# One decoder layer on one core: the left tiles start 128 bytes later, the last output products get written-out places, and the first weights take another queue

## The chip, the cores and the metric

The kernel runs on one core of one Trainium2 chip. A core has five engines that run side by side: TensorE (PE; its weight loads are listed apart as PEld), VectorE (DVE), ScalarE (ACT), GpSimd (POOL) and SyncE (SP), which here only issues transfers. Each executes its own instructions in a fixed order and waits for the others by semaphores. Data lies in an on-chip memory of 128 partitions, matmul results in eight banks of 512 float32 values per partition (PSUM). The metric is the device time of one execution in microseconds (us), as the median of several runs.

## The reference

A hybrid decoder layer on x of 1024 rows (the sequence) by 1024 columns, in float32:

```
xn = rmsnorm(x, attn_norm_g)
proj = xn @ w_in                      # 1024 x 2312, cut into qa ka va qb kb vb f_logit
out_a = swa_sinks_attention(...)      # 8 heads of 64, window 128, 2 key heads, sinks, ALiBi
out_b = forgetting_attention(...)     # 8 heads of 64, causal, bias c[t] - c[s], c = cumsum(log f)
x = x + concat(out_a, out_b) @ w_out
hn = rmsnorm(x, mlp_norm_g)
hid = square(relu(hn @ w_up))         # 1024 x 4096
y = x + hid @ w_down
```

q and k are normalised per head before the scores.

## The kernel before

**Arithmetic.** Every float32 operand of a large product is split in two parts of the type float32r (`split`, line 73, one engine for the high part and one for the remainder), and a product is three matmuls: high by high, high by low, low by high (`mm`, line 70). The stationary operand (the weights, loaded by PEld before each matmul) is the second argument, the streamed operand the third. The up and the down projection use seven block products where eight would be usual.

**Order.** The kernel is written as one program. A planner then simulates a time line and fixes the order of each engine's instructions: it takes what is ready by its own simulation, in program order unless `tc.high_priority` puts a piece ahead (`prep` does). `tc.issue_after(i)` keeps the instructions of a block behind instruction i in that order. So a place in the program is a wish, and `issue_after` is a bound.

**Stages.**
1. *Start* (lines 161 to 196): for each of eight slices k of the inner dimension, SP loads half of xT, the first weights `w_a0`, and the other half (lines 171 to 173); ACT and DVE split x into `xh` and `xl`, DVE and POOL split the weights; PE multiplies into `qps`. `vt`, the tile of small vectors, comes over ACT's own queue (line 105), and ACT's function table is loaded behind it (line 106).
2. *Heads* (lines 203 to 778): a unit is the scores of one head for some rows (`scores_a`, `scores_b`) and, two units later (`DEPTH`), its mixing with v (`mix_a`, `mix_b`: transposes `tpb`, evictions `pth` on ACT and `ptl` on DVE, products `pvb`, the sum `mtb`). `pend` holds the units whose mixing is still to come; `drain(n)` writes the mixing of all but the last n. Between the units lie fillers: projections `ps` of the next heads and the first half of the output projection (`out_first`). `marks` holds the last matmul of each unit's scores. The last heads' rows come in the order `ORDER_END`, 1, 3, 0, 2, in quarters of 256 columns.
3. *Output projection* (lines 789 to 930): eight column tiles dt, each the sum over eight tiles e of the mixed heads. Tiles 0 to 3 are summed early and kept in `part_d`; tiles 4 to 7 come last. Tiles 0 to 6 go through memory (`split_mix` writes `mixs_d`, `load_mix` reads it); tile 7 is split directly from `mtb` (line 708). The products of one dt with one tile are six matmuls of 128x512 (`out_products`). dt 0 and dt 4 have their products with tiles 4 to 6 ahead of the last two units' mixing (lines 863 to 872), then `drain(0)`, then tile 7. `out_finish` adds the part from `part_d`, stores h, and makes the sums and splits that the up projection streams (`bh`, `bl`). For dt 7 the part is loaded into `rr`, a tile of its own.
4. *Up* (`up`, line 978): 16 steps of seven products, 84 matmuls of 128x512 each: weights `wu` stationary, `bh` and `bl` streamed, out to `pu`.
5. *Down* (`down`, line 1102): weights `wx` stationary, `hx` streamed, out to `pd`, in sets of two tiles (`down_set`), 24 matmuls of 128x512 a set. `FIRST` says that the first and third set lie left, the second and fourth right; all later ones lie left.

**Where tiles lie.** Pools on the left side grow upwards from the small constants (`cp`), pools on the right grow downwards from the end. Each tile takes its bytes per partition, rounded up to 32. Ahead of the left tiles stand 2176 bytes of the system's own and, in cp, ident 512, ident_b 256, ones1 32, vt 160 (144 rounded up), nsnk, gqk, rstd and ep2 32 each, rqk 192, nm_a and dn_a 256 each, dn_b 128, mask_b 256, rt and the two of `rsqrt` 32 each, and before 256: together 4704, which is 18 x 256 + 96. `xh`, `xl` and all tiles of zl (mix, wos, wu, hx, wx and others) have sizes that are multiples of 256, so all start at 96 in a step of 256 bytes (the weights of the projections, 1568 bytes each, turn through all multiples of 32). The right side ends at 229,344, 895 x 256 + 224, and so the tiles of ap1 (qk, v) and zr (`bh`, `bl`, the right sets of the down stage) start at 224. In ap2 small tiles lie between the large ones: the tiles of k (`k1`, `k2z`), `pth`, `ptl` and the scores start at 192, the tiles of q (`q1`) at 64.

Of the kernel before, what the change touches and what calls it, by code (L numbers as in the profile page):

```python
# [8 lines left out]
F32 = mybir.dt.float32  # L9
# [7 lines left out]
P = 128  # L17
# [3 lines left out]
NT = S // P  # L21
HD = 64
NH = 8
# [30 lines left out]
def hybrid_layer(  # L54
# [13 lines left out]
    nc = tc.nc  # L68

    def mm(out, lhsT, rhs, start, stop):  # L70
        return nc.tensor.matmul(out, lhsT, rhs, start=start, stop=stop)  # L71
# [20 lines left out]
    cp = ctx.enter_context(tc.tile_pool(name="cp", bufs=1))  # L92
# [10 lines left out]

    vt = cp.tile([P, 36], F32, name="vt")
    nc.scalar.dma_start(vt, vecs)
    nc.scalar.preload_act_table_set("natural_log_exp_and_others")
    ga, gm, vec, bfb, snk = (
# [32 lines left out]
    at = ExitStack()  # L140
    ap1 = at.enter_context(tc.tile_pool(name="ap1", bufs=1, side="right"))
    ap2 = at.enter_context(tc.tile_pool(name="ap2", bufs=1, side="right"))
    maskd = ap2.tile([P, P], F32, tag="mt", name="maskd", bufs=2)
    nc.gpsimd.memset(maskd, 0.0)
# [23 lines left out]
    for k in range(KT):  # L168
        xr = ap2.tile([P, S], F32, tag="s", name="xr", bufs=NS)
        wr, wh, wl = w_tiles()  # L170
        nc.sync.dma_start(xr[:, halves[0]], xT[k * P : (k + 1) * P, halves[0]])
        nc.sync.dma_start(wr[:, :384], w_a0[:, k, :])
        nc.sync.dma_start(xr[:, halves[1]], xT[k * P : (k + 1) * P, halves[1]])
# [54 lines left out]
    def qknorm(x, nh, tlo, thi, r=None):  # L228
# [8 lines left out]
        ss, r0, u = (  # L237
            ap2.tile([P, 16], F32, tag=tag, name=tag, bufs=2)[:, : n * nh]
            for tag in ("ss", "sr0", "su")
# [16 lines left out]
        if r is None:  # L256
            rv = ap2.tile([P, 16], F32, tag="r", name="r", bufs=2)[:, : n * nh]
            rv = th(rv)
        else:
            rv = r[:, tlo:thi, :]  # L260
# [32 lines left out]
    marks = []  # L293

    def paced():
        return tc.issue_after(marks[-1]) if marks else nullcontext()
# [126 lines left out]
    def forget_gates():  # L423
# [31 lines left out]
        )  # L455
        offs = ap2.tile([NH * NT, 1], F32, name="offs")
        nc.vector.tensor_copy(offs, off[: NH * NT, 0:1])
# [167 lines left out]
    def scores_b(p, qp, h):  # L625
        q1, k1, k2, cb = heads[p, "q"][h], heads[p, "k1", h], k2_of[h], heads[p, "cb", h]
        probs = []
        for i in (2 * qp, 2 * qp + 1):
# [4 lines left out]
            )  # L633
            nm = ap2.tile([P, 4], F32, tag="nm", name="nmb", bufs=4)
            dn = ap2.tile([P, 4], F32, tag="dn", name="dnb", bufs=4)
            qs = q1[:, i * P : (i + 1) * P]
# [34 lines left out]
    def mix_b(probs, p, qp, h):  # L671
        r = slice(h * HD, (h + 1) * HD)
        pv = pa.tile([P, 512], F32, tag="pv", name="pvb", bufs=2)
        for b in range(qp + 1):
# [18 lines left out]
            for par in range(2):  # L693
                st = heads[p, "v", h][:, 2 * b + par, :]
                mm(pvo, st, hv[:, :, 1 - par, :], b == 0 and par == 0, False)
                mm(pvo, st, lv[:, :, 1 - par, :], False, diag and par == 1)
        tmp = ap2.tile([HD, 512], F32, tag="cmb", name="tmpb", bufs=1)
# [11 lines left out]

    qkb = {}  # L710
    mh, ml, mixt = {}, {}, {}
    pend = []
# [5 lines left out]
    def drain(n):  # L718
        while len(pend) > n:
            prep(pend.pop(0))  # L720
# [87 lines left out]
    def load_mix(e):  # L808
        mix_tiles(e)
        nc.sync.dma_start(mixt[e].bitcast(F32), mixs_d[e].rearrange("c p s -> p c s"))  # L810
# [50 lines left out]
    fill(True)  # L861
    load_mix(6)
    ahead_of = []
    for dt in (0, 4):
        w = out_weights(dt, 4)

        ps = first_banks() if dt == 0 else [
            pa.tile([P, 512], F32, tag="sc", name=f"po{c}", bufs=2) for c in range(2)
        ]
        with paced():  # L870
            out_products(ps, w, range(4, 7))
        ahead_of.append((dt, ps, w))
    drain(0)
    for dt, ps, w in ahead_of:
        out_products(ps, w, [7])
# [25 lines left out]
    def out_finish(dt, ps):  # L901
        t, gain = dt % 4, gm[:, dt : dt + 1]
        h = slot(f"w{2 + dt // 4}", "h", [S]) if dt < 7 else rr
        part["load"] = nc.sync.dma_start(h, part_d[dt])
        for c, cs in enumerate((left, right)):
# [381 lines left out]
```

## Time and profile before

| | us |
|---|---|
| median of 3 runs | 1126.16 (1122.52 to 1127.7) |
| profiled execution, its own time | 1124.34 |
| its span, from the first to the last instruction | 1122.6 |
| mean granted TensorE clock | 0.998 |

The profile comes from one further execution. Its span is cut into the busy times of each engine; idle time of an engine is put down to what released it at its end (a transfer, another engine's result). A matmul's listed duration reaches from its start to its modelled end and overlaps the next one; what counts in a dense stretch is the distance from one start to the next. The chain of waits follows the work that ended last backwards, from each instruction to what it waited for. By stages: the start reaches to about 40 us, heads and fillers to about 464, the rest of the output projection to about 512, up to 813, down to the end.

### The profile page before, as it was taken

To read this page: it belongs to the slowest core of one execution; us is meant where nothing else is said; L and a number is where in the kernel's file an instruction comes from. 1 tells how busy PE (TensorE), PEld (TensorE's weight loads), DVE (VectorE), ACT (ScalarE), POOL (GpSimd) and SP (SyncE) were. 2 spreads that over 40 slices of the span, in tenths; PEclk is the share of its full clock that TensorE was granted. 3 is DMA by queue.
4 is the path that set the end of the run, shared out by engine and by line. 5 is a ranking of instruction groups with operands and counts; after the bars stand their busy time and mean duration, and the time that the engine had idled before them with its cause. 6 is when DMAs were issued, how large, how long until landed. Compare 5 with 4: busy or idle time off the path is not lost.

```text
span 1122.6 us, 15570 instructions
## 1 busy us (share of the span) xinstructions
PE 1098.7 (98%) x5551; PEld 937.5 (84%) x5551; DVE 765.4 (68%) x1311; ACT 575.4 (51%) x1013; POOL 361.0 (32%) x338
## 2 busy tenths in 40 slices
PE   9999998999999999899999999999999999999998
PEld 8999988799997888777888887888888888888886
DVE  7476665765667577699867677855575876674395
ACT  5567557766677656455454534344444433333331
POOL 4751613335434545124232323222221222222100
PEclk9999999999999999999999999999999999999999
DMA  9311302314438656473454544335699786665523
GB/s 312 124 36 37 95 24 59 96 29 142 153 120 312 203 182 219 168 236 131 173 194 169 196 151 159 134 121 194 227 392 351 258 299 244 216 230 205 173 95 113
DMA packets 95710, 195.68 MB, mean 174 GB/s; under 512 B 7136, under 2 KB 19088, under 8 KB 95632
## 3 DMA queue, kind: packets, MB, share of 16 engines
q1 hardware_dynamic: 95488, 194.66, 49.6%
q8 instruction: 44, 0.72, 0.3%
q14 instruction: 34, 0.28, 0.1%
q10 hardware_dynamic: 144, 0.02, 0.0%
HBM read 141.61 MB, written 53.04 MB: 173 GB/s over the span
## 4 chain that ended last, share of the span: by engine, by line
PE 83%; DVE 7%; issue 4%; DMA 4%; POOL 1%; ACT 1%; SPq 0%; DVEq 0%; ACTq 0%; POOLq 0%
PE pd L71 27%; PE pu L71 27%; PE ps L71 12%; PE po L71 4%; PE qps L71 3%; PE spb L71 3%; PE pvb L71 2%; PE tpb L683 2%; PE sp L71 1%; DVE ptl L360 1%; DMA mixs_d<-mixs 1%; DVE sb L647 1%; DVE bl L78 1%; PE pv L71 1%; DMA wr<-in_w_b_dram 1%
## 5 line engine op out<-in xcount | busy, mean ns | idle before, releaser
L71 PE MATMUL pd<-hx,wx 128*128 128x512 f32 x1344 | 304.9, 389 | 0.0
L71 PEld LDWEIGHTS pd<-hx,wx 128*128 128x128 f32 x1344 | 252.3, 188 | 52.4
L71 PE MATMUL pu<-bh,wu 128*128 128x512 f32 x896 | 281.6, 395 | 0.8 <-ACT wu L75 0.8
L71 PEld LDWEIGHTS pu<-bh,wu 128*128 128x128 f32 x896 | 168.8, 188 | 40.7 <-ACT wu L75 1.2
L71 PE MATMUL pu<-bl,wu 128*128 128x512 f32 x448 | 176.9, 395 | 0.5 <-DVE bl L78 0.5
L75 ACT CAST hx<-hr 128x1024 fp32r<-128x1024 f32 x56 | 59.0, 1054 | 176.2 <-PE pd L71 171.3
L78 POOL TENSOR_TENSOR wx<-wda,wx 128x1024 fp32r<-128x1024 f32 x24 | 64.5, 2687 | 197.0 <-ACT wx L75 197.0
L78 DVE TENSOR_TENSOR hx<-hr,hx 128x1024 fp32r<-128x1024 f32 x56 | 72.7, 1305 | 73.5 <-ACT hx L75 73.4
L71 PE MATMUL ps<-wh,xh 128*128 128x384 f32 (+1 forms) x320 | 110.2, 345 | 0.3 <-ACT qkb L600 0.3
L71 PE MATMUL ps<-wh,xl 128*128 128x384 f32 (+1 forms) x320 | 109.3, 342 | 0.0
L71 PE MATMUL ps<-wl,xh 128*128 128x384 f32 (+1 forms) x320 | 109.1, 342 | 0.0
L71 PEld LDWEIGHTS pu<-bl,wu 128*128 128x128 f32 x448 | 84.4, 188 | 21.1 <-DVE bl L78 0.9
L71 PE MATMUL po<-mix,wos 128*128 128x512 f32 x384 | 95.8, 400 | 3.7 <-DMA mix<-mixs_d 1.6
L78 POOL TENSOR_TENSOR wu<-wus,wu 128x512 fp32r<-128x512 f32 x32 | 48.0, 1501 | 133.4 <-ACT wu L75 133.4
L71 PEld LDWEIGHTS po<-mix,wos 128*128 128x128 f32 x384 | 70.9, 190 | 18.3 <-DMA mix<-mixs_d 1.8
L75 ACT CAST wu<-wus 128x512 fp32r<-128x512 f32 x64 | 39.0, 618 | 79.4 <-PE pu L71 76.0
L78 POOL TENSOR_TENSOR wu<-wur,wu 128x512 fp32r<-128x512 f32 x32 | 43.3, 1354 | 88.2 <-ACT wu L75 88.2
L360 DVE TENSOR_TENSOR ptl<-tpb,pth 128x512 fp32r<-128x512 f32 (+1 forms) x80 | 50.0, 632 | 25.9 <-ACT pth L359 25.2
L965 DVE TENSOR_TENSOR ht<-hb 128x512 f32<-128x512 f32 x32 | 21.8, 722 | 64.7 <-ACT hb L1020 64.7
L78 POOL TENSOR_TENSOR wl<-wr,wh 128x384 fp32r<-128x384 f32 (+1 forms) x47 | 49.9, 1076 | 48.8 <-ACT wh L75 36.9
L75 ACT CAST wx<-wda 128x1024 fp32r<-128x1024 f32 x56 | 58.3, 1044 | 7.2 <-DMA wda<-in_w_d_dram 6.6
L71 PEld LDWEIGHTS ps<-wh,xh 128*128 128x128 f32 x320 | 60.4, 189 | 1.1 <-ACT qkb L600 0.6
(218 smaller groups left out, 2058.4 us busy)
## 6 DMA issues: line engine op xcount, KB each, us to landing
wda<-in_w_d_dram SPq DMA_DIRECT2D x34, 1024.0 KB, 9.0
hr<-hid_d SPq DMA_DIRECT2D x56, 512.0 KB, 5.8
wur<-in_w_u_dram SPq DMA_DIRECT2D x32, 512.0 KB, 4.4
hid_d<-ht SPq DMA_DIRECT2D x16, 1024.0 KB, 4.3
hid_d<-hb SPq DMA_DIRECT2D x16, 768.0 KB, 3.6
mixs_d<-mixs SPq DMA_DIRECT2D x14, 512.0 KB, 3.4
mix<-mixs_d SPq DMA_DIRECT2D x7, 1024.0 KB, 8.7
wr<-in_w_b_dram SPq DMA_DIRECT2D x32, 192.0 KB, 2.4
```

Source lines behind the costliest of these rows:

```text
L71: return nc.tensor.matmul(out, lhsT, rhs, start=start, stop=stop)
L75: hi_eng.copy(hi, src)
L78: lo_eng.tensor_tensor(out=lo, in0=src, in1=hi.bitcast(F32), op=ALU.subtract)
L360: nc.vector.tensor_tensor(out=lo[:, cols], in0=pt[:, cols], in1=hi[:, cols].bitcast(F32), op=ALU.subtract)
L647: nc.vector.tensor_tensor_reduce(out=pr[:, c * 512 : c * 512 + n], in0=sp[:, :n], in1=cb[:, c * 512 : c * 512 + n], scale=1.0, scalar=3e38 ...
L683: nc.tensor.transpose(tp[:, c0 : c0 + P], probs[qi][:, kb * P : (kb + 1) * P], ident)
L965: eng.tensor_tensor(out=out, in0=a, in1=b, op=ALU.subtract)
```

## The change

```diff
--- before.py
+++ after.py
@@ -101,9 +101,10 @@
     ones1 = cp.tile([P, 1], F32, name="ones1")
     nc.vector.memset(ones1, 1.0)
 
-    vt = cp.tile([P, 36], F32, name="vt")
-    nc.scalar.dma_start(vt, vecs)
-    nc.scalar.preload_act_table_set("natural_log_exp_and_others")
+    vt = cp.tile([P, 68], F32, name="vt")
+    nc.scalar.dma_start(vt[:, :36], vecs)
     ga, gm, vec, bfb, snk = (
         vt[:, a:b] for a, b in ((0, 8), (8, 16), (16, 20), (20, 28), (28, 36))
     )
@@ -140,6 +141,8 @@
     at = ExitStack()
     ap1 = at.enter_context(tc.tile_pool(name="ap1", bufs=1, side="right"))
     ap2 = at.enter_context(tc.tile_pool(name="ap2", bufs=1, side="right"))
+    ap3 = at.enter_context(tc.tile_pool(name="ap3", bufs=1, side="right"))
     maskd = ap2.tile([P, P], F32, tag="mt", name="maskd", bufs=2)
     nc.gpsimd.memset(maskd, 0.0)
     nc.gpsimd.affine_select(
@@ -169,7 +172,9 @@
         xr = ap2.tile([P, S], F32, tag="s", name="xr", bufs=NS)
         wr, wh, wl = w_tiles()
         nc.sync.dma_start(xr[:, halves[0]], xT[k * P : (k + 1) * P, halves[0]])
-        nc.sync.dma_start(wr[:, :384], w_a0[:, k, :])
+        (nc.sync if k else nc.scalar).dma_start(wr[:, :384], w_a0[:, k, :])
+        if k == 0:
+            nc.scalar.preload_act_table_set("natural_log_exp_and_others")
         nc.sync.dma_start(xr[:, halves[1]], xT[k * P : (k + 1) * P, halves[1]])
         split(wh[:, :384], wl[:, :384], wr[:, :384], nc.vector, nc.gpsimd if k else nc.vector)
         for cs in halves:
@@ -235,7 +240,7 @@
         xv = x[:, tlo:thi, :w]
         nc.gpsimd.tensor_tensor(out=sqv, in0=xv, in1=xv, op=ALU.mult)
         ss, r0, u = (
-            ap2.tile([P, 16], F32, tag=tag, name=tag, bufs=2)[:, : n * nh]
+            ap3.tile([P, 16], F32, tag=tag, name=tag, bufs=2)[:, : n * nh]
             for tag in ("ss", "sr0", "su")
         )
         nc.vector.tensor_reduce(
@@ -254,7 +259,7 @@
         nc.vector.tensor_tensor(out=u, in0=u, in1=ss, op=ALU.mult)
         na = nh + (2 if r is not None else 0)
         if r is None:
-            rv = ap2.tile([P, 16], F32, tag="r", name="r", bufs=2)[:, : n * nh]
+            rv = ap3.tile([P, 16], F32, tag="r", name="r", bufs=2)[:, : n * nh]
             rv = th(rv)
         else:
             rv = r[:, tlo:thi, :]
@@ -453,7 +458,7 @@
             off[: NH * NT, 0:1], before.rearrange("p h t -> p (h t)"),
             cum[:, P - 1 : P], True, True,
         )
-        offs = ap2.tile([NH * NT, 1], F32, name="offs")
+        offs = ap3.tile([NH * NT, 1], F32, name="offs")
         nc.vector.tensor_copy(offs, off[: NH * NT, 0:1])
         nc.vector.tensor_scalar(
             out=cum, in0=cum, scalar1=offs[:, 0:1], scalar2=None, op0=ALU.add
@@ -631,8 +636,8 @@
                 [P, S if i > 3 else 512], F32, tag="s" if i > 3 else "u", name="sb",
                 bufs=NS if i > 3 else NU,
             )
-            nm = ap2.tile([P, 4], F32, tag="nm", name="nmb", bufs=4)
-            dn = ap2.tile([P, 4], F32, tag="dn", name="dnb", bufs=4)
+            nm = ap3.tile([P, 4], F32, tag="nm", name="nmb", bufs=4)
+            dn = ap3.tile([P, 4], F32, tag="dn", name="dnb", bufs=4)
             qs = q1[:, i * P : (i + 1) * P]
             for c in range((nk + 511) // 512):
                 n = min(512, nk - c * 512)
@@ -693,7 +698,8 @@
             for par in range(2):
                 st = heads[p, "v", h][:, 2 * b + par, :]
                 mm(pvo, st, hv[:, :, 1 - par, :], b == 0 and par == 0, False)
-                mm(pvo, st, lv[:, :, 1 - par, :], False, diag and par == 1)
+                pe = mm(pvo, st, lv[:, :, 1 - par, :], False, diag and par == 1)
+        ended.append(pe.ins)
         tmp = ap2.tile([HD, 512], F32, tag="cmb", name="tmpb", bufs=1)
         nc.scalar.copy(tmp[:, :256], pv[HD:, :256])
         mt = ap2.tile([P, 256], F32, tag="mt", name="mtb", bufs=2)
@@ -708,6 +714,8 @@
             split(mh[7][r, ms], ml[7][r, ms], mt[r, :], nc.scalar, nc.vector)
 
     qkb = {}
+    ended = []
     mh, ml, mixt = {}, {}, {}
     pend = []
 
@@ -860,17 +868,26 @@
         heads_b(p)
     fill(True)
     load_mix(6)
     ahead_of = []
     for dt in (0, 4):
-        w = out_weights(dt, 4)
         ps = first_banks() if dt == 0 else [
             pa.tile([P, 512], F32, tag="sc", name=f"po{c}", bufs=2) for c in range(2)
         ]
-        with paced():
-            out_products(ps, w, range(4, 7))
-        ahead_of.append((dt, ps, w))
+        ahead_of.append((dt, ps, out_weights(dt, 4)))
+    def beside(n, mark, *es):
+        _, ps, w = ahead_of[n]
+        with tc.issue_after(mark):
+            out_products(ps, w, es)
+    beside(0, marks[-1], 4, 5)
+    beside(0, ended[-1], 6)
+    beside(1, ended[-1], 4)
+    drain(1)
+    beside(1, ended[-1], 5)
     drain(0)
+    beside(1, ended[-1], 6)
     for dt, ps, w in ahead_of:
         out_products(ps, w, [7])
 
@@ -901,7 +918,8 @@
     def out_finish(dt, ps):
         t, gain = dt % 4, gm[:, dt : dt + 1]
         h = slot(f"w{2 + dt // 4}", "h", [S]) if dt < 7 else rr
-        part["load"] = nc.sync.dma_start(h, part_d[dt])
+        with tc.issue_after(part["load"].ins) if dt == 7 else nullcontext():
+            part["load"] = nc.sync.dma_start(h, part_d[dt])
         for c, cs in enumerate((left, right)):
             nc.vector.tensor_tensor(out=h[:, cs], in0=ps[c], in1=h[:, cs], op=ALU.add)
         nc.sync.dma_start(h_d[dt], h)
```

In words:
- **Left tiles.** vt takes 272 bytes instead of 144, with rounding 288 instead of 160; the first 144 are used as before. All left tiles behind it start 128 bytes later, the large ones at 224 in a step of 256.
- **Right tiles.** The small tiles of ap2 move to a new pool ap3 beside it: `ss`, `sr0`, `su`, `r`, `offs`, `nm` and `dn`, 384 + 128 + 32 + 256 = 800 bytes. Of these, 288 (`offs`, `nm`, `dn`) stood above the tiles of `pth`, `ptl` and `k1`, 128 more (`r`) above those of `q1`, and 384 more above the rest. Names, numbers of buffers and the instructions on them stay.
- **First weights.** The slice k = 0 of `w_a0` is loaded over ACT's queue, behind vt; ACT's table load comes behind it. The other seven slices stay on SP's queue.
- **Output products.** `mix_b` notes its last matmul in `ended`. The weights of dt 0 and dt 4 are made first; then the products are bound one by one: dt 0 with tiles 4 and 5 behind the last scores; dt 0 with tile 6 and dt 4 with tile 4 behind the end of the third-last unit's mixing; dt 4 with tile 5 behind the second-last unit's; dt 4 with tile 6 behind the last unit's. Tile 7 follows for both as before.
- **Load for dt 7.** `rr` is loaded behind the load of dt 3's part, which the loop issues just before.

## The prediction

> **What bounds the kernel now.** I read the page's busy shares first.
>
> ```profile
> PE 1098.7 (98%) x5551; PEld 937.5 (84%) x5551; DVE 765.4 (68%) x1311; ACT 575.4 (51%) x1013; POOL 361.0 (32%) x338
> ```
>
> PE is idle for 1122.6 - 1098.7 = 23.9 us in all. A gain above that can only come from matmuls that follow each other more closely. So the second view is the chain of waits in order of time, which holds the two long stages as single pieces (start, length, matmuls):
>
> ```profile
> 512.40 181.77 PE pu L71 x781
> ...
> 695.88 117.12 PE pu L71 x504
> ...
> 813.01 300.64 PE pd L71 x1326
> ```
>
> Both stages run 128x512 matmuls of one type, with a weight load before each, and nothing but PE is in these pieces. Yet pu takes (181.77 + 117.12) / 1285 = 232.6 ns from one start to the next, and pd 300.64 / 1326 = 226.7 ns. That is 5.9 ns for each pu matmul, and the page's durations (395 against 389 ns) say the same:
>
> ```profile
> L71 PE MATMUL pd<-hx,wx 128*128 128x512 f32 x1344 | 304.9, 389 | 0.0
> ...
> L71 PE MATMUL pu<-bh,wu 128*128 128x512 f32 x896 | 281.6, 395 | 0.8 <-ACT wu L75 0.8
> ```
>
> What differs is where the operands lie. In pd the streamed tile hx and the weights wx lie on one side of the memory, both at byte 96 of a 256-byte step, or both at 224. In pu the streamed bh and bl are right (224) and the weights wu left (96): 128 bytes apart. The timeline of PE settles which feature counts, start and length of 22 matmuls in the first set of tiles of the down stage (left with left, at 96) and in the second (right with right, at 224):
>
> ```profile
> 813.08 5.17 PE L71 MATMUL pd<-hx,wx 128*128 128x512 f32 x22
> ...
> 818.55 5.15 PE L71 MATMUL pd<-hx,wx 128*128 128x512 f32 x22
> ```
>
> Taking off one duration of 0.39 leaves 21 steps: 227.6 and 226.7 ns. So 224 is as good as 96 when both operands have it. And two operands of one side that are 128 bytes apart (k at 192, q at 64) are not at 226.7; three starts of the last heads, no wait between them:
>
> ```profile
> 421.55 0.39 PE L71 MATMUL spb<-k1b,q1b 128*128 128x512 f32 x1
> 421.78 0.39 PE L71 MATMUL spb<-k2z,q1b 128*128 128x512 f32 x1
> 422.02 0.40 PE L71 MATMUL pvb<-pth,vb 128*128 128x256 f32 x2
> ```
>
> The two steps take 0.47 us, 235 ns each (to 5 ns, by rounding). I therefore read the rate as set by the **distance** of the two operands modulo 256 bytes, not by the side and not by the place.
>
> The third view is PE's timeline where the last heads and the output projection meet, with the windows around it (us; busy time of PE, PEld, DVE, ACT, POOL; clock; DMA share; GB/s).
>
> ```profile
> 434.12 0.38 PE L71 MATMUL pvb<-ptl,vb 128*128 128x256 f32 x1 [0.58 <-DVE ptl L360]
> ...
> 435.54 0.39 PE L71 MATMUL pvb<-ptl,vb 128*128 128x256 f32 x1 [0.35 <-DVE ptl L360]
> ...
> 437.98 3.01 PE L71 MATMUL po<-mix,wos 128*128 128x512 f32 x12
> ...
> 440.94 1.55 PE L71 MATMUL po<-mix,wos 128*128 128x512 f32 x6
> ...
> 443.24 1.31 PE L71 MATMUL po<-mix,wos 128*128 128x512 f32 x5
> ...
> 447.88 0.38 PE L71 MATMUL pvb<-ptl,vb 128*128 128x256 f32 x1 [0.18 <-DVE ptl L360]
> ...
> 451.69 3.34 PE L71 MATMUL po<-mix,wos 128*128 128x512 f32 x8 [1.58 <-DMA mix<-mixs_d]
> ...
> 461.62 1.64 PE L71 MATMUL po<-mix,wos 128*128 128x512 f32 x6 [1.40 <-ACT mix L75]
> ...
> 463.95 0.50 PE L71 MATMUL po<-mix,wos 128*128 128x512 f32 x1 [0.69 <-ACT wos L75]
> ```
>
> ```profile
> 450.00:456.00 6.00, 4.42 (x17) 3.64 (x16) 1.52 (x3) 1.06 (x3) 0.00 (x0) 0.72 0.38 157
> ...
> 464.00:512.40 48.40, 47.12 (x204) 37.86 (x204) 47.03 (x63) 26.59 (x45) 15.65 (x11) 1.00 0.68 228
> ...
> 512.40:694.00 181.60, 181.60 (x781) 147.27 (x782) 131.98 (x195) 86.49 (x111) 54.92 (x38) 1.00 0.46 167
> ```
>
> From 438 to 464 PE waits 0.18 + 1.58 + 1.40 + 0.69 = 3.85 us. After the wait of 1.58 the granted clock is 0.72 over six us, which costs 6 x 0.28 = 1.7 us (the eight matmuls at 451.69 have (3.34 - 0.39) / 7 = 0.42 us from start to start). Together 5.5 us. Up to 512.4 DVE (47.03 of 48.4) and PE (47.12) are equally full, so a start that comes earlier there passes on to the end; a faster pu matmul before 512.4 does not.
>
> **The change, part by part.**
>
> **Places of the tiles.** vt grows by 128 bytes, so every left tile behind it goes from 96 to 224. The right tiles of ap1 and zr stay at 224. In ap2 the small tiles leave: 288 bytes above the k and pth tiles (192 + 288 = 480, that is 224), 128 more above q1 (64 + 416 = 480), 384 more above sq. All large tiles of both sides then stand at 224. Terms:
> - pu from 512.4 on: 1285 x 5.9 ns = **7.5 us**, at pd's rate. The other engines must keep up with a stage 2.5% shorter: in its first part DVE is busy 73%, ACT 48%, POOL 30%, DMA 0.46, so nothing is late next. Ends: 0 (the distance is not the cause) and 7.5 (pd's rate is the fastest steady one here).
> - pd, po and the projections ps: both operands are left, the distance stays. Nothing.
> - Heads: 96 + 60 matmuls of 128x512 (spb; pv), by the rows at 421.55 about 8 ns each, 1.2 us. PE waits for evictions in between, so I take half, **0.6**. For the 256-wide ones no aligned row exists; 8 ns saved or lost on some 100 that nothing hides gives ends of -1 and +2.
>
> One rule speaks against this term. The Trainium skill ("SBUF — State Buffer", section "Who interferes with whom"; "TensorE: Matmul & The Clock Gate", Part 2) gives TensorE two independent read ports, one for the moving operand and one for the weight load, and says that loading the next weights takes no read bandwidth from the running matmul. By that rule alone the first term would be 0; the rows at 512.40 and 813.01, which differ by 2.5% for one instruction, don't fit it, unless the cause is something else between them (the first rival).
>
> **Output products.** Before, the 24 products of tiles 4 and 5 stood behind the last scores (rows 437.98 to 443.24). Now 12 stay, 6 go behind the third-last unit's end, 6 behind the second-last's, and the 6 of dt 4 with tile 6 behind the last unit's end. What each does:
> - The six behind the last unit take 6 x 0.227 = 1.36 us, just where PE waits 1.40 for the last unit's sums and splits (row 461.62): 1.3 gained.
> - dt 0 then ends ahead of dt 4, so its weight slot is free for dt 1's split while six products of dt 4 still run: of the 0.69, 0.6 gained.
> - mix 6 comes when its transfers end, whatever PE does:
>
> ```profile
> 436.05 5.80 DMA mixs_d<-mixs
> ...
> 443.94 2.74 DMA mixs_d<-mixs
> ...
> 446.74 4.90 DMA mix<-mixs_d
> ```
>
>  That is 451.64. Twelve products leave the time before it and six to twelve can come back, so the wait of 1.58 and the slow clock after it (3.3 together) may go or stay: half, 1.6.
> - The units between 441 and 449 lose twelve matmuls as cover. Uncovered blocks waited 0.58 and 0.35 (434.12, 435.54); I take two to three more of these: -1.2. Behind such a waiting pvb matmul stand all of PE's next transposes, and DVE and ACT wait for those.
>
> Sum **2.3 us**. Ends: +4.6 (all 5.5 less 0.9 of uncovered blocks), and -2 (1.4 longer wait for mix 6 for six products not put back, another slow window of 1.7, 0.8 of uncovered blocks, less the 1.9 of the first two).
>
> **First weights on ACT's queue.** Start and landing, then who waited:
>
> ```profile
> 1.71 4.41 DMA xr<-in_xT_dram
> ```
>
> ```profile
> 1.24 0.42 SPq L172 DMA_DIRECT2D wr<-in_w_a_dram  x1
> ...
> 1.23 1.28 ACT L106 ACT_TABLE_LOAD   x1 [1.23 <-PEq L1270]
> ...
> 3.84 0.72 ACT L176 ACTIVATE xh<-xr,vt 128x512 fp32r<-128x512 f32 x1 [1.32 <-DMA vt<-in_vecs_dram]
> ...
> 5.35 0.94 PE L71 MATMUL qps<-wh,xh 128*128 128x384 f32 x4 [0.47 <-DVE wh L77]
> ...
> 6.91 0.97 PE L71 MATMUL qps<-wh,xh 128*128 128x384 f32 x4 [0.62 <-ACT xh L176]
> ```
>
> SP issues the second half of xr 0.47 us earlier (1.24 for 1.71); ACT issues wr at about 1.2, as before. The table load moves behind it and ends near 2.9, still ahead of vt at 3.84: nothing. All later loads of SP move up by as much. PE is dense from 6.91, which the second half sets, so up to 0.47 could be won; but wr now shares the engines with it, and wh (row 5.35) may be late instead. I take **0.3**, ends -0.5 (wr as late as xr is early) and 0.8 (0.47, and 0.3 if wh comes early too).
>
> **rr's load** now waits for dt 3's load:
>
> ```profile
> 447.16 0.46 SPq L904 DMA_DIRECT2D rr<-part_d  x1
> ...
> 491.83 0.32 SPq L904 DMA_DIRECT2D h<-part_d  x1
> ...
> 492.20 0.90 SPq L948 DMA_DIRECT2D wur<-in_w_u_dram  x2
> ...
> 493.21 5.68 SPq L907 DMA_DIRECT2D h_d<-h  x2
> ...
> 501.57 1.28 DVE L906 TENSOR_TENSOR rr<-po,rr 128x512 f32<-128x512 f32 x2
> ```
>
> It moves from 447.16 to 492 or 493. DVE needs it at 501.57; a load issued at 446.74 took 4.90 for twice the bytes. Nothing, if it stands ahead of the stores; behind them (498.9) it would land some 1.2 us late. Ends -1.2 and 0.
>
> **Sum.** 7.5 + 0.6 + 2.3 + 0.3 = 10.7 us. The profiled execution took 1124.34 us (span 1122.6 and 1.74 around it): 1113.6. The median of the runs shown, 1126.16, is 1.8 above it, so on the median I forecast **1115.5**. With every term at its good end it is 7.5 + 2 + 4.6 + 0.8 = 14.9 less, 1111.3; at its bad end, but with pu's 7.5, 2.8 less, 1123.4.
>
> **Rivals.**
> - **Distance is not the cause.** pu is the only stage whose operands come from two sides; if that costs the 5.9 ns, the shift changes nothing there or in the heads. Left are 2.3 + 0.3: 1123.5. Against it stands the step of 235 ns with both on the right. Chance 0.10.
> - **Place, not distance (slower).** If a streamed tile at 224 is what is slow, pu is slow for bh and bl, and the shift takes hx and mix from 96 to 224 as well: 1326 + 384 matmuls x 5.9 ns = 10.1 us lost, pu unchanged, 2.6 gained elsewhere: 1133.7. It decides as soon as pd loses more than 2 ns a matmul. Against it: the 22 matmuls at 818.55, at 224 and 226.7 ns. Chance 0.03.
> - **The products are placed badly.** pu gains, but the units run uncovered and PE waits longer for mix 6: 7.5 + 0.6 + 0.3 - 2 = 6.4 leaves 1119.8, and rr late by 1.2 makes it 1121.0. For it: the two uncovered waits; against: the six products that fit the last wait. Chance 0.17.
> - **Another engine bounds the up stage**, and half of pu's gain goes: 1119. Nothing on PE's side of 512.4 to 813 waits now. Chance 0.04.
>
> **How the numbers follow.** The forecast holds 0.66. A measurement of this kernel tells about 0.5% (5.6 us) from no change. Faster by more: 0.66, 0.12 of the third rival, 0.03 of the fourth, 0.81. Within: 0.10 of the first, 0.05 and 0.01, 0.16. Slower: 0.03. The range takes the sum's good end and the runs' spread of 2 us below it, 1109, and reaches up past the third rival to 1122; the first and the second stay out.
>
> **What would show it.** Right: the chain's pu pieces at 226 to 227 ns a matmul, pd's unchanged; spb's steps near 227; no wait for mix L75 ahead of the last products; the clock 1.00 around 450. Wrong: pu still at 232, or pd slower; pvb waiting often for ptl between 440 and 450; DVE idle ahead of rr. I would be most wrong if the new waits moved the whole order of the heads, which no row here can show.

## The result and the profile after

The changed kernel takes 1114.35 us (median of 6 runs, 1111.95 to 1117.57), against 1127.09 (6 runs, 1122.52 to 1129.03) of the kernel before in the same measurement: a ratio of 0.989, with a 95% interval of 0.9866 to 0.9914. Its profiled execution took 1114.11 us, with a span of 1112.4, 10.2 below the span before.

The busy shares of the kernel after (the row that the prediction showed first):

```profile
PE 1088.7 (98%) x5551; PEld 935.4 (84%) x5551; DVE 768.4 (69%) x1311; ACT 572.9 (52%) x1013; POOL 361.2 (32%) x338
```

PE does the same 5551 matmuls in 10.0 us less, and its idle time stays: 1112.4 - 1088.7 = 23.7 us, before 23.9. So on balance the gain lies in busy time: in the matmuls' spacing, and in one place in the clock (below). The waits that go there are made up for by others, most of them earlier: ahead of the first matmuls with real data 1.54 us for 0.47 + 0.62, and between 40 and 60 us 0.43 + 0.35 for none. The chain of waits of the kernel after, its two long stages (start, length, matmuls):

```profile
509.47 177.36 PE pu L71 x781
...
688.55 114.29 PE pu L71 x504
...
802.84 300.57 PE pd L71 x1326
```

The same 1285 pu matmuls take 291.65 us, before 298.89: 227.0 ns each for 232.6. The pd matmuls are unchanged (300.57 for 300.64), though their left tiles moved by 128 bytes as well. The groups by line show it too, 390 ns a matmul for 395:

```profile
L71 PE MATMUL pu<-bh,wu 128*128 128x512 f32 x896 | 276.6, 390 | 0.7 <-ACT wu L75 0.7
```

The other place is the end of the heads. PE's timeline of the kernel after, from its first product of tile 4 to its first product of dt 1:

```profile
438.78 3.01 PE L71 MATMUL po<-mix,wos 128*128 128x512 f32 x12
...
444.34 0.38 PE L71 MATMUL pvb<-pth,vb 128*128 128x256 f32 x1 [0.73 <-ACT pth L364]
...
445.07 0.39 PE L71 MATMUL pvb<-ptl,vb 128*128 128x256 f32 x1 [0.34 <-DVE ptl L365]
...
447.53 0.39 PE L71 MATMUL pvb<-ptl,vb 128*128 128x256 f32 x1 [0.34 <-DVE ptl L365]
...
461.23 9.13 PE L71 MATMUL po<-mix,wos 128*128 128x512 f32 x39 [0.69 <-ACT wos L75]
```

From 438.78 to 461.23 are 22.45 us; before, 437.98 to 463.95 were 25.97. The waits in it fell from 3.85 to 0.73 + 0.34 + 0.34 + 0.69 = 2.10: those for mix 6 (1.58) and for the last splits (1.40) are gone, those for pvb blocks that no other work covers grew by 1.2, the one for wos is as long as before. The windows there (us; busy time of PE, PEld, DVE, ACT, POOL; clock; DMA share; GB/s) give a full clock where it was 0.72, which is the other 1.7 us:

```profile
450.00:456.00 6.00, 6.00 (x37) 5.26 (x36) 3.55 (x7) 2.75 (x6) 0.38 (x2) 1.00 0.38 154
```

The account of the span, the same matmul looked up in both traces:

| stretch | before | after | gained |
|---|---|---|---|
| start and heads, to the first product of tile 4 | 437.98 | 438.78 | -0.8 |
| to the first product of dt 1 | 25.97 | 22.45 | 3.5 |
| to the dense part of pu | 48.45 | 48.24 | 0.2 |
| the two pieces of pu | 298.89 | 291.65 | 7.2 |
| pd | 300.64 | 300.57 | 0.1 |

The sum is 10.2, as the spans differ. Open are the cause of the 7.2 (distance, place or side), which parts bring the 3.5, and where the -0.8 comes from.

### The profile page after: what moved, and what is told of

The parts are those of the page before. It is cut to its first block, busy times and chain, and to the rows that moved or that the text cites. A ratio compares the mean times of both kernels' runs of the same rounds, so it can differ in the third digit from the quotient of the medians.

```text
span 1112.4 us, 15573 instructions
## 1 busy us (share of the span) xinstructions
PE 1088.7 (98%) x5551; PEld 935.4 (84%) x5551; DVE 768.4 (69%) x1311; ACT 572.9 (52%) x1013; POOL 361.2 (32%) x338
## 4 chain that ended last, share of the span: by engine, by line
PE 80%; DVE 9%; DMA 4%; issue 3%; ACT 2%; POOL 1%; SPq 0%; ACTq 0%; DVEq 0%; POOLq 0%
PE pd L71 27%; PE pu L71 26%; PE ps L71 12%; PE po L71 4%; PE spb L71 3%; PE pvb L71 2%; PE tpb L688 2%; PE sp L71 1%; DMA xq<-in_x_dram 1%; DVE ptl L365 1%; DMA xr<-in_xT_dram 1%; PE pv L71 1%; PE tpa L524 1%; DVE sb L652 1%; DMA h_d<-h 1%
## 5 line engine op out<-in xcount | busy, mean ns | idle before, releaser
L71 PE MATMUL pu<-bh,wu 128*128 128x512 f32 x896 | 276.6, 390 | 0.7 <-ACT wu L75 0.7
L71 PE MATMUL pu<-bl,wu 128*128 128x512 f32 x448 | 174.4, 390 | 0.8 <-DVE bl L78 0.8
```

## The experiments

Each edit below is against the kernel before or against the changed one, as said. Most of them leave PE's order of instructions as it is, so a stretch can be compared matmul by matmul. The runs of the kernel before that belong to each had medians from 1125.54 to 1125.75 us. Where no median is given, the time is that of one execution.

### The place of the left side alone: left128, left64, left96

Only the size of vt is changed in the kernel before; no instruction moves, the right tiles stay at 224:

```diff
-    vt = cp.tile([P, 36], F32, name="vt")
-    nc.scalar.dma_start(vt, vecs)
+    vt = cp.tile([P, 68], F32, name="vt")     # left128; left64: 52, left96: 60
+    nc.scalar.dma_start(vt[:, :36], vecs)
```

By that the large left tiles stand at 224 (left128), 160 (left64) and 192 (left96): 0, 64 and 32 bytes from the right ones, for 128 in the kernel before.

> Only vt is wider, so that every left tile starts 128 bytes later; every instruction and its order is that of the kernel before. If the distance of the streamed operand and the weights sets the rate of the up stage (theory), its 1285 matmuls from 512 us on come at 226.7 to 227 ns instead of 232.6 and the span is 7.2 to 7.6 us shorter, with nothing else moved. If the gain of the up stage came from the small tiles' move on the right or from another order (rival), the up stage stays at 232.6 and the time at that of before.

> vt is widened by 64 bytes: left tiles at 160, right ones at 224, 64 apart; order as before. If only equal places modulo 256 are fast, the up stage stays near 232; if what matters is the place modulo 128 or 64, 64 bytes apart gives 226.7 (modulo 64) or stays slow (modulo 128). The down stage, left with left, stays at 226.7 in each case.

> vt is widened by 96 bytes: left tiles at 192, right ones at 224, 32 bytes apart; order as before. If the loss grows with the distance (3.9 ns at 64, 5.9 at 128), the up stage comes at 227 to 230 ns; if any distance costs the same step, at 230.6 or above.

left128: 1117.4 us (4 runs, 1116.28 to 1117.98), ratio 0.9934 (0.991 to 0.9957). left64: 1120.77. left96: 1125.89. The pieces of the chain of waits, left128 first:

```profile
503.13 186.76 PE pu L71 x821
...
691.61 114.29 PE pu L71 x504
...
805.90 300.57 PE pd L71 x1326
```

```profile
511.00 179.05 PE pu L71 x781
...
691.77 117.60 PE pu L71 x504
...
809.37 300.72 PE pd L71 x1326
```

```profile
512.66 182.50 PE pu L71 x781
...
696.88 117.60 PE pu L71 x504
...
814.47 300.73 PE pd L71 x1326
```

The second pu piece, 504 matmuls in each, has nothing but PE in it: 226.8 ns a matmul in left128, 233.3 in left64 and left96 (before, 232.4). The first gives 227.5, 229.3 and 233.7 (before, 232.7), one after the other. The pd matmuls, both of whose operands move together, stay at 226.7 to 226.8 with the left side at 224, 160 or 192. So 128 bytes of shift alone make the whole of pu's gain. 64 bytes gain a third of it over both pieces, all of it in the first; 32 bytes gain nothing. The full rate is there only where the two operands stand at equal places; there is no steady fall with the distance. Neither of the two outcomes expected of left64 came (226.7, or near 232): in its first piece the steps of bl are 226.1 ns and those of bh 230.4, in its second 233.6 and 233.2, with the same places. What decides at 64 bytes was not found.

The layout also bounds the step. In left128 the operands of each pu matmul are an odd multiple of 256 bytes apart, those of each pd matmul an even one, and both have 226.7 to 226.9 ns where nothing waits. So a distance of 256 bytes costs nothing, and those of 32, 64 and 128 do.

### The other side moved: right128

A pad at the end of the right side takes the right tiles down to 96, where the left ones stand:

```diff
+    pad_p = ctx.enter_context(tc.tile_pool(name="pad_p", bufs=1, side="right"))
+    pad = pad_p.tile([P, 32], F32, name="pad")
+    nc.vector.memset(pad, 0.0)
```

> 128 unused bytes at the end of the right side bring the right tiles to 96 and leave the left ones at 96. Distance theory: up stage at 226.7 to 227 ns, as with the left shift. If the place 224 of one operand were what counts, or only a shift of the left side helped, the up stage would stay at 232 or the down stage would change from 226.7.

It took 1118.58 us, and its chain of waits has

```profile
504.72 186.58 PE pu L71 x821
...
693.02 114.29 PE pu L71 x504
```

the same 226.8 ns with both operands at 96 as left128 has with both at 224. Between these two places there is no difference.

### One side, two places: pd_apart

If it is the distance, it must also slow two operands of one side. In the changed kernel a gap of 128 bytes is put ahead of the later left slots of the up stage, which the down stage uses as well. The first set of pd then has both operands left and 128 bytes apart, as have 888 of the pd matmuls in all, and 384 matmuls of pu have their weights 128 bytes from what is streamed:

```diff
+    slot("gap", "gap", [32])
```

> The changed kernel with an unused tile of 128 bytes on the left side ahead of the loads of the up stage. In the down stage 888 of 1344 matmuls then stream hx from 96 with weights at 224, both on the left side; the other 456 keep 224 and 224. In the up stage 384 have weights at 96 and 960 at 224. Distance theory: these 888 take about 232 ns and the rest 226.7, the down stage is 4 to 5 us longer; in the up stage the 384 take 232, the rest 226.7, 2 us more. Rival (only operands from two sides slow each other): the down stage stays at 226.7 throughout.

It took 1123.09 us (span 1121.4, 9.0 above the changed kernel's). PE's timeline of pd_apart, a run of matmuls in the first set of pd (left with left, apart), in the second (right with right, at equal places) and in the third (left with left, apart):

```profile
806.25 5.29 PE L71 MATMUL pd<-hx,wx 128*128 128x512 f32 x22
...
811.61 5.15 PE L71 MATMUL pd<-hx,wx 128*128 128x512 f32 x22
...
817.30 5.06 PE L71 MATMUL pd<-hx,wx 128*128 128x512 f32 x21
```

Without the last one's 0.39 us these are (5.29 - 0.39) / 21 = 233.3 ns, 226.7, and 4.67 / 20 = 233.5. The whole piece of pd took

```profile
805.72 306.56 PE pd L71 x1326
```

6.0 us more than the 300.57 of the changed kernel, for 888 slowed matmuls: 6.7 ns each. The pieces of pu show the same within one run:

```profile
509.98 178.82 PE pu L71 x781
...
690.51 115.20 PE pu L71 x504
```

They are 2.4 us longer than in the changed kernel, 6.2 ns for each of the 384 matmuls whose weights are apart; 2 us were expected. Within these pieces the steps of the matmuls with weights at 96 average 232.3 to 232.9 ns, those with weights at 224 average 226.8 to 227.0. So pd has the slow rate, with both operands on the left; and left128, right128 and the changed kernel have the fast rate with the operands on two sides. The side doesn't matter. This was the test that the first rival of the prediction could have won.

### The right side's small tiles alone: right_small

Of the change only the pool ap3 is put into the kernel before, so that the heads' tiles on the right all stand at 224:

```diff
+    ap3 = at.enter_context(tc.tile_pool(name="ap3", bufs=1, side="right"))
...
-            nm = ap2.tile([P, 4], F32, tag="nm", name="nmb", bufs=4)
-            dn = ap2.tile([P, 4], F32, tag="dn", name="dnb", bufs=4)
+            nm = ap3.tile([P, 4], F32, tag="nm", name="nmb", bufs=4)
+            dn = ap3.tile([P, 4], F32, tag="dn", name="dnb", bufs=4)
```

> Only the small tiles' move on the right side: all tiles of the heads at 224, the left ones at 96, order as before. Theory from the traces so far: nothing; the steps of the 512-wide scores stay at 234 ns, the up stage at 232.6, and the stretch from 60 to 430 us within 0.5 us of before. Rival (the prediction's term): these steps come at 227, the stretch 0.6 to 1.2 us shorter.

It took 1124.28 us, with the span of the kernel before (1122.6). The scores of the heads by line in right_small:

```profile
L71 PE MATMUL spb<-k1b,q1b 128*128 128x512 f32 x48 | 20.7, 430 | 0.6 <-DVE nmb L651 0.6
...
L71 PE MATMUL spb<-k2z,q1b 128*128 128x512 f32 x48 | 19.0, 395 | 0.0
```

and in the changed kernel:

```profile
L71 PE MATMUL spb<-k1b,q1b 128*128 128x512 f32 x48 | 20.7, 431 | 0.6 <-DVE nmb L652 0.6
...
L71 PE MATMUL spb<-k2z,q1b 128*128 128x512 f32 x48 | 18.9, 395 | 0.0
```

Both durations are as before (430 and 396 ns), and the step from k1b to k2z is 235 ns in the median of both traces (before, 234). The small tiles' move gained nothing here. Why these matmuls keep to some 235 ns wherever the tiles stand was not found. Something like it shows in the po products, whose operands stand at equal places in every kernel here: in the changed kernel's run of twelve behind the last scores (438.78) the steps are 315 ns once and then 224 to 236, and from 465 us on, where they are not broken by other work, 226.7 on average. A pair of scores always stands between other matmuls; whether that is the reason was not tested. Equal places alone don't bring the fast rate in this stage.

The move even seems to cost something at the start. Where the right side is untouched (before, left128, left64, left96, places_only), PE's matmul of q1 and k1 that stands at 58.06 in the kernel before begins between 57.98 and 58.48 us. Where it is moved, with the first weights on SP's queue, it begins at 58.72 (ordered7), 59.35 (sp_queue), 59.54 (right_small) and 59.60 (right128). It waits there for a chain that begins with the last load of xq, which is issued at 29.4 to 30.1 us in the five and at 30.3 to 31.3 in the four. In right_small the first product of tile 4 then comes at 438.84, for 437.98 before: 0.9 later, as in the changed kernel (438.78); sp_queue has 439.47, ordered7 439.22. Of the five, left64, left96 and places_only stand at 437.62 to 438.11; left128 has 439.09, but its clock is 0.83 from 340 to 350 us, which costs 1.7. One trace each, and the nearest two of the groups at 58 us are only 0.24 apart, so this is likely and not shown. Why these loads would take longer was not found.

### The products' places: places_only and old_places

places_only puts the output products' places, with `ended`, into the kernel before; old_places takes them out of the changed kernel. The core of the edit, one way and the other:

```diff
-        with paced():
-            out_products(ps, w, range(4, 7))
...
+    beside(0, marks[-1], 4, 5)
+    beside(0, ended[-1], 6)
+    beside(1, ended[-1], 4)
...
```

> Only the output products' places are changed. Theory from the two traces: the stretch from the first product with tile 4 (437.98) to dt 1's first product (463.95) shrinks by 3.5 us, the wait of 1.58 for mix 6, the 1.40 for the last unit and the slow clock go, three waits of 0.3 to 0.7 for evictions come; the up stage stays at 232.6 ns. Span 3 to 3.7 shorter. Rival: the gain there was the placement's only with the shifted tiles or by luck of the clock window: under 1.5 us.

> The changed kernel with the output products' places as before. Theory: the waits for mix 6 (1.6) and for the last unit (1.4) are back, and the slow clock if its window falls so: 2 to 4 us more than the changed kernel. Rival: under 1 us more.

places_only: 1122.86 us (10 runs, 1119.78 to 1123.87), ratio 0.9971 (0.9957 to 0.9984), so 3.3 us gained (1.8 to 4.8). old_places: 1118.37 (4 runs, 1117.58 to 1120.25), ratio 0.9938 (0.9918 to 0.9958); that is 4.1 above sp_queue (1114.28), which ran with it and has the new places, but also the first weights on another queue. Against the two ratios of the changed kernel itself (0.989 and 0.9912, other measurements) old_places takes 2.9 to 5.4 us more. PE's timeline of places_only:

```profile
437.92 3.06 PE L71 MATMUL po<-mix,wos 128*128 128x512 f32 x12
...
460.58 9.59 PE L71 MATMUL po<-mix,wos 128*128 128x512 f32 x41 [0.69 <-ACT wos L75]
```

and of old_places:

```profile
441.34 3.25 PE L71 MATMUL po<-mix,wos 128*128 128x512 f32 x12
...
455.88 3.48 PE L71 MATMUL po<-mix,wos 128*128 128x512 f32 x8 [2.16 <-DMA mix<-mixs_d]
...
465.82 1.66 PE L71 MATMUL po<-mix,wos 128*128 128x512 f32 x6 [1.40 <-ACT mix L75]
...
468.15 2.11 PE L71 MATMUL po<-mix,wos 128*128 128x512 f32 x8 [0.68 <-ACT wos L75]
```

The stretch is 22.66 us with the new places and the tiles as before, 26.81 with the old places and the tiles moved. In old_places the waits of the kernel before are back, and with them the low clock. Two windows with the old places, of old_places and of left64:

```profile
448.00:460.00 12.00, 9.63 (x54) 8.10 (x53) 5.05 (x10) 4.26 (x9) 0.88 (x5) 0.86 0.37 131
```

```profile
448.00:460.00 12.00, 9.09 (x56) 7.68 (x54) 6.78 (x13) 4.45 (x10) 0.74 (x4) 1.00 0.31 125
```

The clock is 0.86 over twelve us (12 x 0.14 = 1.7 us lost) in the one, 1.00 in the other. With the old places the stretch took 26.0 to 26.8 us in five traces (before, left128, right128, left96, old_places), all with the low clock, and 24.4 and 24.8 in two (left64, right_small) without it. With the new places it took 22.2 to 22.8 in seven traces, none with the low clock there. So the places gain about 2 us of waits, and 1.7 more where the clock would have fallen. places_only passes this on: it is 3.4 us ahead of the kernel before at dt 1's first product (460.58 for 463.95) and 3.2 at the end (span 1119.4 for 1122.6).

### The wait for wos: ordered7

The wait of 0.69 ahead of dt 1 stayed, although dt 0 was to be through well ahead of dt 4. In the trace of the changed kernel tile 7's products of dt 0 and dt 4 alternate, so that dt 0's weight slot comes free only near the end. In ordered7 (sp_queue, below, and this edit) those of dt 4 follow those of dt 0:

```diff
-    for dt, ps, w in ahead_of:
-        out_products(ps, w, [7])
+    for n, (dt, ps, w) in enumerate(ahead_of):
+        with tc.issue_after(last7) if n else nullcontext():
+            last7 = out_products(ps, w, [7])
```

> The changed kernel with the first weights on the sync engine's queue, and the products of dt 4 with tile 7 bound behind those of dt 0. Theory: dt 0 ends 0.7 us earlier, its weight slot is free while dt 4's six products run, so the wait of 0.69 for dt 1's weights goes; the span is 0.6 to 0.9 us under that of the run with the sync engine's queue, if VectorE, which is full from there to 512 us, starts as much earlier. Rival: VectorE or another order of the following products takes it back: no gain, 0 to 0.5 us more.

PE's timeline of ordered7 around dt 1's first products, and then its waits from 438 to 515 us (us in total, times, longest):

```profile
457.50 5.01 PE L71 MATMUL po<-mix,wos 128*128 128x512 f32 x19
...
462.83 7.34 PE L71 MATMUL po<-mix,wos 128*128 128x512 f32 x31 [0.33 <-POOL wos L78]
```

```profile
PE pu L71 <- DVE bl L915: 1.5, 2, 1.2
...
PE pu L71 <- DVE bl L78: 0.6, 1, 0.6
```

The first row ends with four products of dt 1, from 461.44 on, with the high part of its weights: the wait of 0.69 for that part, ACT's, is gone, as expected. The fifth product needs the low part and waits 0.33 for POOL. The first pu matmuls then waited 2.1 us for DVE and 0.2 for ACT, where sp_queue waited 1.1 for ACT and 0.5 for DVE:

```profile
PE pu L71 <- ACT wu L75: 1.1, 1, 1.1
...
PE pu L71 <- DVE bl L78: 0.5, 1, 0.5
```

ordered7 took 1116.82 us (5 runs, 1115.59 to 1117.17), ratio 0.9918 (0.9904 to 0.9932): no better than sp_queue's 0.9897 (0.9875 to 0.9918), and its trace is 0.7 longer (span 1114.2 for 1113.5). What is gained ahead of dt 1 isn't passed on here: from 461.4 to 510.6 us DVE is busy 47.67 us of 49.2 in ordered7, PE 46.50. So the expectation's rival came true (0 to 0.5 us more); that it is DVE that takes the gain back fits these numbers, but no run separates it from the changed order of instructions.

### The first weights' queue and the load for dt 7: sp_queue, rr_early, after_again

sp_queue is the changed kernel with the first weights on SP's queue again and the table load in its old place; rr_early is the changed kernel without the bound on the load for dt 7; after_again is the changed kernel once more.

```diff
-        (nc.sync if k else nc.scalar).dma_start(wr[:, :384], w_a0[:, k, :])
-        if k == 0:
-            nc.scalar.preload_act_table_set("natural_log_exp_and_others")
+        nc.sync.dma_start(wr[:, :384], w_a0[:, k, :])
```

```diff
-        with tc.issue_after(part["load"].ins) if dt == 7 else nullcontext():
-            part["load"] = nc.sync.dma_start(h, part_d[dt])
+        part["load"] = nc.sync.dma_start(h, part_d[dt])
```

> The changed kernel with the first weights on the queue of the sync engine again and the table load where it was. If the ACT queue made the start late (theory: wr landed at 5.12 instead of 4.20, and VectorE's cast of it stands behind eight other instructions), the first matmul is at 5.3 to 5.4 instead of 6.43, and the projections at 60 us stand 0.5 to 1.3 us earlier than in the changed kernel; the end 0.3 to 1.3 us earlier. Rival: the 1.3 us at 60 us comes from the loads' own scatter from run to run, and the time stays within 0.3 us.

> The changed kernel without the bound on the load for dt 7. Theory: the load stands early in the queue again and nothing waits for it in either place; span within 0.3 us of the changed kernel, apart from the scatter. Rival: early, it takes the engines from mix 6's load, which then lands 1 us or more later.

> The changed kernel once more, in the same rounds as the run before. Ratio to the kernel before 0.987 to 0.992. If the start's loss is a matter of the clock's window (theory), its first sixteen matmuls may take 2.9 us as in one trace or 4.2 as in three others; by 60 us the traces are together within 0.3 us in each case.

sp_queue: 1114.28 us (4 runs, 1113.46 to 1115.26), ratio 0.9897 (0.9875 to 0.9918), against 0.989 (0.9866 to 0.9914) and 0.9912 (0.9898 to 0.9926) for the changed kernel in two measurements: no difference that can be told. rr_early: 1114.9, with the same order on PE; its span is 0.8 above the changed kernel's, beyond the 0.3 expected, but its clock is 0.86 from 128 to 140 us, 1.7 us lost far from the edit, and PE doesn't wait for mix 6 in it.

The start of the changed kernel (engine, line, operation), where DVE splits the first weights:

```profile
4.31 1.70 DVE L402 TENSOR_SCALAR ab<-dist 128x256 f32<-128x256 f32 x8
...
5.93 0.35 DVE L77 CAST wh<-wr 128x384 fp32r<-128x384 f32 x1
...
6.43 1.65 PE L71 MATMUL qps<-wh,xh 128*128 128x384 f32 x8 [1.54 <-DVE wh L77]
...
7.92 1.58 PE L71 MATMUL qps<-wl,xh 128*128 128x384 f32 x8
...
59.37 0.39 PE L71 MATMUL sp<-k1a,q1a 128*128 128x256 f32 x1 [0.35 <-DVE q1a L286]
```

and PE's start in sp_queue:

```profile
5.43 0.94 PE L71 MATMUL qps<-wh,xh 128*128 128x384 f32 x4 [0.90 <-DVE wh L77]
...
7.77 1.57 PE L71 MATMUL qps<-wl,xh 128*128 128x384 f32 x8
...
59.35 0.39 PE L71 MATMUL sp<-k1a,q1a 128*128 128x256 f32 x1 [0.36 <-DVE q1a L285]
```

On ACT's queue the weights were issued at 1.23 us, as before, but landed at 5.12 instead of 4.20; then DVE was in the middle of eight small `ab` instructions. PE's first matmul is 1.0 later than in sp_queue, its wait in the middle is gone, and its second pass begins 0.15 later. At 59 us both stand at the same matmul at the same time, since PE waits there for q1, which hangs on later loads (right_small, above). PE's start in after_again:

```profile
6.39 2.90 PE L71 MATMUL qps<-wh,xh 128*128 128x384 f32 x8 [1.52 <-DVE wh L77]
...
9.09 0.84 PE L71 MATMUL qps<-wl,xh 128*128 128x384 f32 x2
```

Here the first eight matmuls came 320 ns apart instead of about 177 (2.90 us for 1.65), so that the second pass begins 1.2 later. The clock is given as 1.00 from 6 to 9.2 us all the same, so it is not shown that this is the clock. Of the five traces with this queue four show it (pd_apart, old_places, rr_early, after_again; the changed kernel's first does not), of the nine with SP's queue none. The loads that PE waits for later hide most of it: the matmul that sp_queue starts at 59.35 comes at 59.37, 59.47, 59.48, 59.92 and 60.86 in the five. Three stand within 0.2 us of it, two don't, though all were expected within 0.3.

## Why the prediction was right

The forecast was 1115.5, the measured time 1114.35. The gain forecast was 10.7 us; it is 10.2 between the two profiles and, by medians, 12.7 in the first measurement and 9.9 in that of after_again. Its steps, one by one:

- **The first term (7.5 us) was right** in size, 7.24 in the trace, and in its cause: moving either side alone brings it (left128, right128), two places on one side bring the loss back (pd_apart), and the place itself is indifferent (both operands at 96, 160, 192 or 224). The first rival (two sides) and the second (place) fall. "Distance" was still too much said. 32 bytes cost as much as 128 and 64 bytes two thirds of it (over both pieces left96 takes 233.5 ns a matmul, left64 230.9, the kernel before 232.6), so in these two dense stages it is equal places that bring the full rate, and the loss doesn't grow steadily with the distance. The Trainium skill's rule that was weighed ("SBUF — State Buffer", "Who interferes with whom"; "TensorE: Matmul & The Clock Gate", Part 2) would give 0 here. The measurement decides: the places of the two operands relative to each other do change the running matmuls' spacing, 232.6 ns to 227.0. What in the hardware does this no run here shows.
- **Nothing for pd, po and ps** held: pd 300.57 for 300.64, and the po steps from 465 us on are 226.7 ns for 226.8.
- **The heads' 0.6 us failed.** The step was to read the two starts of 235 ns as a cost of distance. right_small moved exactly these tiles and the durations stayed; in the changed kernel too. These steps were no evidence for the distance at all: the conclusion drawn from them, that the side isn't the cause, was right by luck, and only pd_apart shows it. The prediction's own rows held the warning: the six po products at 440.94, both operands at 96, come (1.55 - 0.39) / 5 = 232 ns apart.
- **The products' 2.3 us was too small**: 3.5 in the trace, 3.3 by places_only (1.8 to 4.8), and 2.9 to 5.4 by old_places. Three parts of it were off. The wait for mix 6 and the slow clock were taken at half; both went whole (3.3, not 1.6). Of the wait for wos, 0.6 was to go; nothing went, since the products of tile 7 alternate. ordered7 orders them, PE then waits 0.33 for the other part of these weights, and nothing is gained. The uncovered blocks cost 1.2, as said: in the trace 0.73 + 0.34 + 0.34, for 0.18 before.
- **The first weights' +0.3 failed in sign.** The step "ACT issues wr at about 1.2, as before", hence nothing late, left out that the load is slower beside the others and that DVE, in order, has other work by then. It costs 0.2 us of PE's second pass in the profile of the changed kernel and more with the slow start, and nothing that can be told in the time (sp_queue).
- **The load for dt 7 at 0** held, but with 0.1 us to spare: issued at 490.62, landed at 498.57, used at 498.66 without a wait. It took 7.95 us, where the prediction went by 4.90, and DVE came to it 2.9 us earlier than before (501.57).
- **The -0.8 us** up to 438.78 had no term at all: the prediction took the right side's move as free apart from its matmuls. right_small has the same loss without any other part of the change, so it stands most likely there, by loads that come later; with one trace each that isn't shown. A kernel with the left shift and the products' places alone, which leaves the right side as it was, was not run; an estimate from these traces is some 0.8 us below the changed kernel.

In sum the terms and losses missed (0.6, 0.3 and the start's) were nearly made good by the products' extra 1.2. The total was better than its parts, 10.7 forecast and 10.2 in the trace, and that much of it is luck; the 7.5 that carries it is not.

## What to carry to other kernels

Where two stages run the same matmul and one is some 2.5% slower with nothing but TensorE in it, look at the start of the streamed tile and of the weights modulo 256 bytes, and make them equal by a pad on either side; one padded tile at the head of a pool did here what 1285 matmuls needed. A wait of some 2 us on TensorE can cost nearly its length once more through the clock (1.6 to 2.3 us here, in five of seven traces), so work that fits into it is worth more than the wait's length. And ask what waits next before ordering more by hand. Ahead of a stretch in which VectorE is as full as TensorE, the new places brought the whole stretch forward, and the gain came through to the end (places_only); ordered7 took one wait of TensorE's away, and others came in its place.

## What the runs showed of the hardware

- **Equal places.** In the dense pieces of pu and pd, 128x512 matmuls with a weight load before each followed each other at 226.7 to 227.5 ns where streamed operand and weights start at equal places modulo 256 bytes, and, averaged over a piece, at 229.3 to 233.7 ns where they stand 32, 64 or 128 bytes apart, on one side of the memory or on two. For the heads' scores no such effect was seen: about 235 ns with equal places as with unequal ones.
- **The clock falls after short waits, and not always.** With the old places PE waited about equally long for mix 6 in right_small and in left96, first right_small and then left96:

```profile
452.93 2.12 PE L71 MATMUL po<-mix,wos 128*128 128x512 f32 x8 [1.96 <-DMA mix<-mixs_d]
```

```profile
452.23 3.36 PE L71 MATMUL po<-mix,wos 128*128 128x512 f32 x8 [1.97 <-DMA mix<-mixs_d]
```

 After it the eight products took 2.12 us in the one and 3.36 in the other; of the two, left96 alone has a granted clock of 0.86 over the twelve us around it. With the old places the clock fell after waits of 1.58, 1.97, 2.00, 2.16 and 2.31 us and didn't after 1.51 and 1.96, so what decides was not settled. The Trainium skill ("TensorE: Matmul & The Clock Gate", Part 1, "What's actually happening") has a free-running window of about 3.4 us after whose idleness the clock is halved; that it runs free would fit the scatter. If the clock is halved, 0.86 over twelve us is 2 x 0.14 x 12 = 3.4 us of it, the length of one such window; but no wait here was 3.4 us long.
- **The same outside this place.** A window of after_again far from any edit:

```profile
128.00:140.00 12.00, 9.75 (x54) 9.00 (x53) 6.55 (x22) 6.54 (x20) 6.49 (x6) 0.86 0.56 183
```

 costs 12 x 0.14 = 1.7 us there, and it isn't in the changed kernel's first profile, though both are the same program. rr_early has 0.86 in the same twelve us, and left128, right128 and old_places have it from 338 to 350 us. It is the size of differences that one profile cannot assign to an edit.
